# A list scheduler learns that GpSimd and VectorE take turns on two-input SBUF work, and the weight remainders go to VectorE alone

## The chip, the cores and the metric

One core of one Trainium2 chip runs the whole program in one launch. The metric is the device time in microseconds, median of the runs. Engines are named as the profile names them: PE is TensorE, DVE is VectorE, ACT is ScalarE, POOL is GpSimd and SP is SyncE, which here only issues the loads and stores.

## The reference

Two transformer-like blocks are computed in float32 for 256 tokens of 1024 features, with one set of weights each.

```
x = hybrid_layer(x, c, ...)        # block 1
h  = rmsnorm(x, g) * (1 + scale_m) + shift_m ; z = h @ w_in
merged = gate0 * (attention @ wa) + gate1 * (pool_mixer @ wb) + gate2 * (short_conv @ wc)
x = x + gate_m * rmsnorm(merged @ w_out)
x = x + gate_f * rmsnorm(square(relu(h2 @ w_ff1)) @ w_ff2)
...
x = second_block(x, mem, ...)      # block 2
y = concat(spatial_gating(za), moba_attention(q, k, v), conformer_conv(zc)) @ w_out
x = x + rms_norm(y); x = x + rms_norm(memory_cross_attention(...))
x = x + rms_norm(square(relu(h @ w_ff1)) @ w_ff2)
```

Some 160 MB of float32 weights pass through once.

## The kernel before, in words

**Products in three parts.** Each float32 factor is split into a rounded part `hi` (fp32r) and the exact remainder `lo`. A product is `xh*wh + xl*wh + xh*wl`, three matrix products into one PSUM bank. The tokens are two tiles of 128 rows, and the loops run over the tiles `t`, column chunks of 512, and k tiles of 128.

**Weights.** A weight unit is 128 x 1024 (two k tiles of 512 columns, 512 KB). SP loads it into a `raw` buffer, ACT makes `hi` by a copy, and `lo = raw - hi` is a subtraction of two SBUF inputs (`split_unit`). In the page these are `hi_w_...` and `lo_w_...`. Activations are split in the same way from PSUM (`evac_split`).

**The subtraction's engine.** In the kernel before, `split_unit` records the subtraction under `rec.either()`: it belongs to DVE, but POOL may take it where the scheduler finds POOL free long enough before it is due.

**What else is on DVE and POOL.** DVE sums the modulation rows (`G_a`, `S_a`, `GG_a`: 128 x 512 or 128 x 1024), does the attention's maxima, additions and normalisations (`alg`, `ap`, `bp`), the short convolution (`cy`), a part of the 31-tap convolution (`dy`), the residuals (`x0b`, `wG`) and the remainders of activations (`f1rT`, `kz`, `aPT`). POOL does each reciprocal root (`rstd`: an addition of eps, an addition, a power, on 128 x 1), the pooling windows (`s`, `pm`), 30 additions of the 31-tap convolution (`dy<-dy,tap`) and the additions to `merged`.

**What sets the order.** The program is recorded first (`Recorder`); `schedule` then plans thirty passes with a table of costs in microseconds and keeps the best, and each engine's instructions are issued in that fixed order. In `one_pass` every engine has a time at which it is free; an instruction can start when its inputs are made (plus a latency `LAT`), its engine is free, its buffers are free and its PSUM bank is not held. `urgency` turns the PE gaps of one pass into due times for the next. The engines run in order on the chip: what stands at the head of an engine's queue and waits holds up all behind it.

In the plan before, DVE and POOL never hold each other up: a subtraction on DVE is planned with 0.068 + 1024/960 us whatever POOL does. Nearly every instruction has line 1635 of the file in the profile, the line that issues them all, so rows are told apart by tile names.

Of the kernel before, what the change touches and what calls it, by code (L numbers as in the profile page):

```python
# [19 lines left out]
P = 128  # L20
D = 1024
# [23 lines left out]


def _chunk(rows, c, w, per):
    """One column chunk, `per` k tiles a unit."""
    return [(list(range(k, k + per)), c, w) for k in range(0, rows // P, per)]
# [6 lines left out]
def _ff2_units():  # L56
    """For each chunk of 512 rows both column halves."""
    return [([k, k + 1], c, 512) for g in range(8) for c in (0, 512) for k in (4 * g, 4 * g + 2)]
# [49 lines left out]
def _constants():  # L108
# [5 lines left out]
    # a pair of heads' rows of the running sums, and the even and the odd rows  # L114
# [5 lines left out]
    # slopes 2 ** -(h + 1) of a pair's heads: a diagonal times halved and quartered distances  # L120
# [17 lines left out]
class Buf:  # L138
    """A recorded tile; it takes a place of its tag when its first write is scheduled."""
# [11 lines left out]
class View:  # L151
    """A view of a recorded tile; `how` makes it from the tile's access pattern."""
# [17 lines left out]
    def cut(self, n):  # L170
        """the last axis as (axis, n)"""
        ids = self.ids.reshape(self.ids.shape[:-1] + (-1, n))
        if len(self.shape) == 2:
            return self._with(ids, lambda ap: ap.rearrange("p (k t) -> p k t", t=n))
        return self._with(ids, lambda ap: ap.rearrange("p a (k t) -> p a k t", t=n))

    def flat(self):
        """the last two axes as one"""
        ids = self.ids.reshape(self.ids.shape[:-2] + (-1,))
        return self._with(ids, lambda ap: ap.rearrange("p k t -> p (k t)"))  # L180

    def spread(self, shape):
        """stride 0 along the last axis, or along a new middle axis"""
# [14 lines left out]
class Pair:  # L198
    """The rounded part and the exact rest of values, as one index in the second place."""
# [9 lines left out]
class Wide:  # L209
    """Pairs of tiles of 4 k tiles each; one token tile of them."""  # L210
# [8 lines left out]
class At:  # L219
    """One token tile of a view whose last axis is the tokens."""  # L220
# [8 lines left out]
class Op:  # L229
    __slots__ = ("eng", "home", "due", "calls", "costs", "after", "prio", "waits", "ready", "users", "new", "bufs", "banks", "table", "end", "why", "start", "key", "goal", "mean", "boost", "freer")  # L230


class Recorder:
    """Engines whose calls are recorded with what they read and write, and a list
    scheduler that then emits them: each engine takes, of the instructions that are
    ready, the first in the recorded order (with its offset)."""

    # microseconds from the end on one engine to the start on another
    LAT = {"PE": 0.2, "ACT": 0.15, "DVE": 0.15, "POOL": 0.1, "SP": 0.9}
    TO_PE, LOOK, SWITCH = 0.12, 0.25, 1.28  # L240
    # the function tables that serve what not every table has
# [31 lines left out]
    def first(self):  # L273
        """what is recorded here goes ahead of all else, in its order"""
# [5 lines left out]
    def together(self):  # L280
        """products of one accumulation, issued without others between them"""
# [7 lines left out]
    def either(self):  # L289
        """for DVE, or for Pool when that has the time"""  # L290
# [12 lines left out]
    def add(self, eng, calls):  # L303
# [4 lines left out]
        op.costs = {e: sum(self.cost(e, *c) for c in calls) for e in ([eng, "POOL"] if self.flex else [eng])}  # L308
        after, bufs = {}, {}
# [29 lines left out]
        # no write to a tile before the one that takes its place  # L339
# [9 lines left out]
    def cost(self, eng, method, args, kw):  # L349
        """microseconds that an instruction holds its engine"""  # L350
        vs = [v for v in list(args) + list(kw.values()) if isinstance(v, View)]
        n = max(int(np.prod(v.shape[1:])) for v in vs) if vs else 1
        if eng == "PE":
            passes = 2 if method == "matmul" and kw["lhsT"].buf.dtype == F32 else 1
            return passes * (max(int(np.prod(vs[0].shape[1:])) / 2400, 0.107) + 0.0025)
        if eng == "SP":
            return vs[0].shape[0] * n * 4 / 3.6e5
        if eng == "ACT":
            ptr = sum(isinstance(kw.get(k), View) for k in ("bias", "scale", "accum_out"))
            return (0.052 if args[1].buf.tag == "ps" else 0.094) + n / 1200 + 0.093 * ptr  # L360
        if eng == "POOL":
            if method == "memset":
                return 0.035 + 0.000833 * n
            if method == "tensor_scalar":
                return 0.16 + 0.00116 * n
            if method == "tensor_copy":
                return 0.12 + 0.0033 * n
            return 0.3 + 0.165 * n if kw.get("op") == OP.pow else 0.15 + 0.0021 * n
        if method == "reciprocal":
            return 0.068 + 0.0063 * n  # L370
# [5 lines left out]
        return 0.068 + n / rate + 0.061 * ptr  # L376

    def schedule(self):
        """The recorded instructions in the order in which they are to be issued:
        the best of some passes, each with the urgencies that follow from the last."""  # L380
# [26 lines left out]
    def urgency(self, out):  # L407
        """latest starts with which PE would go without a gap; they order the other engines"""
        end = gap = 0.0
        for t, op in out:  # L410
            if op.home == "PE":
# [3 lines left out]
                if t - end > 0.1:  # L415
                    # the chain that PE has waited for goes sooner
# [31 lines left out]
    def one_pass(self):  # L448
        engs = list(self.real)
        free = {e: 0.0 for e in engs}  # L450
        dma_free, table = 0.0, ["exp"]
        slots = {tag: [(0.0, place, None, None) for place in places] for tag, places in self.slots.items()}
        pending = {t: list(o) for t, o in self.order.items()}
        todo = {e: [] for e in engs}  # all that came before is scheduled
# [9 lines left out]
        def placed(op):  # L464
            """when all new tiles of op can have a place, or None"""
            r, got = 0.0, {}
            for b in op.new:
                f, line = slots[b.tag], pending[b.tag]
                # every tile that comes before in the recorded order keeps a place
# [6 lines left out]
        def turn(op):  # L476
            """a bank of PSUM serves one engine at a time"""
            return max((t + lat(o, op.eng) for b in op.banks for o, t in b.held.items() if o != op.eng), default=0.0)

        while len(out) < len(self.ops):  # L480
            best = None
            for e in engs:
                cands = []
                for op in todo[e] if e != "SP" else sorted(todo[e], key=lambda o: o.key)[:24]:
                    r = placed(op) if op.new else 0.0
                    if r is not None:
                        cands.append((max(r, op.ready, free[e], turn(op)), op))
                if e == "POOL":
                    for op in todo["DVE"]:
                        if "POOL" in op.costs and op.due is not None:  # L490
                            r = max(placed(op) or 0.0, op.ready, free[e])
# [31 lines left out]
            else:  # L523
# [4 lines left out]
                op.end = free[e] = t + c  # L528
            op.start = t
# [18 lines left out]
def tile_two_blocks(ctx: ExitStack, tc: tile.TileContext, a: dict, out: bass.AP):  # L548
# [6 lines left out]
    # a pool for each place, so that the schedule says which one a tile takes  # L555
# [54 lines left out]
    def split_unit(raw, n, name, pieces=1):  # L610
        hi = work([P, D], "k4", f"hi_{name}", F32R)
        lo = work([P, D], "k4", f"lo_{name}", F32R)
        for i in range(pieces):
            s = slice(i * n // pieces, (i + 1) * n // pieces)
            act.activation(hi[:, s], raw[:, s], AF.Copy)
            with rec.either():
# [3 lines left out]
    # pieces of work that go between the weight units  # L620
# [31 lines left out]
    def use(u, xT, ps, first, last, xk=None, apart=False):  # L652
        """ps += x @ unit; xT(k) or xT [P, 2, k, P]"""
# [19 lines left out]
    def rstd(means, name, eps=None):  # L673
        """(the sum of the means + eps) ** -0.5"""
# [14 lines left out]
    def squares(parts, name):  # L689
        """each row's sum of squares over a piece, divided by the length D of the rows"""  # L690
# [8 lines left out]
    def evac_split(dst_hi, dst_lo, src, scale=None):  # L699
        """src (times scale) into its rounded part and the exact rest"""  # L700
# [14 lines left out]
    def to_T(src, dst, nb, name, scale=None):  # L715
        """src [P tok, nb*128] f32 -> dst [P, 2, nb, P]"""
# [5 lines left out]
    def to_T_gain(src, dst, g, name, halves=(0, 1)):  # L722
        """src [P tok, 1024], transposed, times g along the features -> dst"""
# [14 lines left out]
    # ================= start: mem, modulation =================  # L738
    mem = [work([P, 4, 256], "k4", f"mem{h}") for h in range(2)]  # features on the partitions
# [18 lines left out]
    # silu(c)  # L758
# [5 lines left out]
    # keys of one head keep only its half of a pair's rows; the other half stays zero  # L764
# [4 lines left out]
    def sums_on_partitions(src, n, name):  # L769
        """the sums of src's n * 128 columns over its partitions, on the partitions"""  # L770
# [11 lines left out]
    def mem_gain(k):  # L782
        """a k tile of both token tiles times its gains"""
# [4 lines left out]
    def mem_stats():  # L788
        """each token's mean square: over the k tiles first, then over the partitions"""
# [14 lines left out]
    def chunk(wname, u0, nu, xT, name, n=512, after=None):  # L804
        """x @ one column chunk for both token tiles, the first ahead of the second"""
# [35 lines left out]
    def mod_vector(j, name, gname=None, plus1=False, raw=None):  # L841
        """One of the six vectors on all partitions, as pieces of work: shift, or
        gate * g, or (1 + scale) * g. The partial sums of each partition's rows
        come first, then the sum over the partitions."""
# [40 lines left out]
    def mod_column(j, half, name, bias, gname=None):  # L885
        """half of the features of shift, or of (1 + scale) * g, on the partitions,
        as pieces of work"""
# [47 lines left out]
    def norm_shift(t, xG, r, S, name):  # L935
        """(xG * r + S) transposed and split; xG is overwritten"""
# [7 lines left out]
    # x * rstd(x) transposed, its first 512 features and its last  # L944
# [36 lines left out]
    # ================= block 1: w_in =================  # L981
    # forget gates and pooling input
# [28 lines left out]
    def log_sigmoid():  # L1011
        """min(z, 0) - log1p(u), u = exp(-|z|);
        log1p(u) = log(w) * u / (w - 1) with w = 1 + u, and u where w is 1"""
# [23 lines left out]
    def running_sums(t):  # L1037
        """cumq [token, head], and cumT [head, token] with the rounded parts in the
        first rows and the rest from row 32 on, even heads apart from odd"""
# [24 lines left out]
    def pooling(t):  # L1064
        """windowed sums by doubling, channels on partitions"""
# [57 lines left out]
    # the first chunks start with the features that are ready first  # L1123
# [157 lines left out]
    # ================= projections back to the residual =================  # L1281
    def proj(wname, xT, name, after, xk=None):
        """x @ w for 1024 columns, the first token tile ahead of the second"""
# [56 lines left out]
    def junction(t, y, x, G, g, name):  # L1340
        """x += G * y * rstd(y); (x * g) transposed and split, and rstd(x), which
        goes into the next outputs"""
# [343 lines left out]
```

## Time and profile before

| what | value |
|---|---|
| time, median of 3 runs | 862.42 us (861.46 to 863.27) |
| span of the profiled execution, first to last instruction | 856.9 us |
| median of the runs over that span | 5.5 us |
| PE busy | 790.5 us, 92% |
| DVE busy | 603.1 us, 70% |
| ACT busy | 482.2 us, 56% |
| POOL busy | 274.3 us, 32% |
| mean granted PE clock | 0.976 |
| HBM traffic | 163.64 MB read, 192 GB/s over the span |

The profiled execution's own total is not listed beside its span, so the three runs stand for it. A group's row reads: line, engine, operation, output<-inputs, shapes, count, then busy time and the mean of one in ns, then the idle time of the engine just before these instructions and who ended it.

### The profile page before, as it was taken

Reading aid. Unit: us, or ns where it says so; the run is one execution under the profiler, and the core shown is the slowest. Engines: PE = TensorE matmul, PEld = TensorE weight load, DVE = VectorE, ACT = ScalarE, POOL = GpSimd, SP = SyncE. Lnnn points to the kernel's source line nnn. Section 1 sums busy time; section 2 is a strip of 40 time slices with the busy share of each in tenths; the row PEclk is TensorE's granted clock in tenths of the full one; section 3 lists DMA queues with packets and bytes.
Section 4 is the critical chain, followed back from the end, with each engine's and each line's share of the span. In section 5 each row is a group of like instructions: output and inputs, shape, how many; then the busy total and the mean of one; then the engine's idle time right before and its main releaser. Section 6 shows DMA issues by size and latency. Waiting matters only on the chain.

```text
span 856.9 us, 10705 instructions
## 1 busy us (share of the span) xinstructions
PE 790.5 (92%) x3722; PEld 650.2 (76%) x3722; DVE 603.1 (70%) x814; ACT 482.2 (56%) x802; POOL 274.3 (32%) x227
## 2 busy tenths in 40 slices
PE   6998779999999789999999996879999999999997
PEld 4887667777877567888887785768787788888885
DVE  6798898977786986544454869898777954445413
ACT  6763745654454546555554785568576854545522
POOL 4143944543434544000000669364543400000000
PEclk9999999999999899999999999889999999999999
DMA  8998435556784566455556452314254555555511
GB/s 320 398 378 298 168 120 197 200 198 220 293 319 163 194 243 241 168 178 190 197 197 204 152 197 75 124 49 172 101 194 166 197 203 178 185 202 179 185 31 49
DMA packets 49630, 165.39 MB, mean 193 GB/s; under 512 B 5412, under 2 KB 6564, under 8 KB 49576
## 3 DMA queue, kind: packets, MB, share of 16 engines
q1 hardware_dynamic: 49576, 164.71, 54.7%
q8 instruction: 29, 0.48, 0.2%
q14 instruction: 25, 0.20, 0.1%
HBM read 163.64 MB, written 1.05 MB: 192 GB/s over the span
## 4 chain that ended last, share of the span: by engine, by line
PE 61%; DVE 19%; ACT 6%; DMA 5%; issue 5%; POOL 3%; SPq 0%; DVEq 0%; POOLq 0%; ACTq 0%
PE f2y L1635 10%; PE f2f L1635 10%; PE f1y L1635 9%; PE f1f L1635 8%; PE kv L1635 4%; PE wo L1635 3%; DMA raw_w_in<-in_w_in_dram 3%; DVE lo_w_in L1635 3%; PE bcg L1635 2%; DVE dy L1635 2%; PE xo L1635 2%; DVE GG_a L1635 2%; PE xq L1635 1%; PE xA L1635 1%; DVE G_a L1635 1%
## 5 line engine op out<-in xcount | busy, mean ns | idle before, releaser
L1635 DVE TENSOR_TENSOR lo_w_ff<-raw_w_ff,hi_w_ff 128x1024 fp32r<-128x1024 f32 x115 | 144.2, 1258 | 126.9 <-ACT hi_w_ff L1635 105.0
L1635 ACT ACTIVATE hi_w_ff<-raw_w_ff 128x1024 fp32r<-128x1024 f32 x128 | 134.7, 1061 | 109.6 <-DMA raw_w_ff<-in_w_ff_dram 78.4
L1635 POOL TENSOR_TENSOR lo_w_in<-raw_w_in,hi_w_in 128x1024 fp32r<-128x1024 f32 (+1 forms) x27 | 68.2, 2534 | 77.3 <-ACT hi_w_in L1635 42.3
L1635 PE MATMUL f1y<-hi_w_ff,f1rT 128*128 128x512 f32 x256 | 81.5, 399 | 3.4 <-DVE f1rT L1635 3.4
L1635 PE MATMUL f1f<-hi_w_ff,h2T 128*128 128x512 f32 x256 | 80.9, 397 | 0.3 <-DVE h2T L1635 0.3
L1635 ACT ACTIVATE hi_w_in<-raw_w_in 128x1024 fp32r<-128x1024 f32 (+1 forms) x66 | 67.3, 1035 | 24.2 <-DMA raw_w_in<-in_w_in_dram 16.3
L1635 PE MATMUL f2f<-hi_w_ff,h5T 128*128 128x512 f32 x256 | 80.0, 393 | 0.0
L1635 PE MATMUL f2y<-hi_w_ff,f2rT 128*128 128x512 f32 x256 | 79.6, 392 | 0.0
L1635 DVE TENSOR_TENSOR lo_w_in<-raw_w_in,hi_w_in 128x1024 fp32r<-128x1024 f32 (+1 forms) x39 | 64.5, 1661 | 7.5 <-ACT hi_w_in L1635 6.6
L1635 PEld LDWEIGHTS f1y<-hi_w_ff,f1rT 128*128 128x128 f32 x256 | 48.1, 191 | 13.9 <-DVE f1rT L1635 4.2
L1635 PEld LDWEIGHTS f1f<-hi_w_ff,h2T 128*128 128x128 f32 x256 | 48.0, 190 | 10.2 <-DVE h2T L1635 0.6
L1635 PEld LDWEIGHTS f2y<-hi_w_ff,f2rT 128*128 128x128 f32 x256 | 47.5, 188 | 9.4
L1635 PEld LDWEIGHTS f2f<-hi_w_ff,h5T 128*128 128x128 f32 x256 | 47.4, 188 | 9.5 <-DVE h5T L1635 0.2
L1635 POOL TENSOR_TENSOR o_m<-o_ss,e 128x1 f32<-128x1 f32 x2 | 0.4, 190 | 165.6 <-ACT junk L1635 165.6
L1635 PE MATMUL f1y<-lo_w_ff,f1rT 128*128 128x512 f32 x128 | 50.5, 394 | 0.0
L1635 PE MATMUL f1f<-lo_w_ff,h2T 128*128 128x512 f32 x128 | 50.1, 392 | 0.0
L1635 PE MATMUL f2f<-lo_w_ff,h5T 128*128 128x512 f32 x128 | 49.9, 390 | 0.0
L1635 PE MATMUL f2y<-lo_w_ff,f2rT 128*128 128x512 f32 x128 | 49.9, 390 | 0.0
L1635 PE MATMUL kv<-hi_w_xkv,memT 128*128 128x512 f32 x128 | 42.4, 414 | 5.8 <-ACT hi_w_xkv L1635 5.7
L1635 POOL TENSOR_TENSOR lo_w_ff<-raw_w_ff,hi_w_ff 128x1024 fp32r<-128x1024 f32 x13 | 35.5, 2739 | 34.8 <-ACT hi_w_ff L1635 27.3
L1635 PEld LDWEIGHTS kv<-hi_w_xkv,memT 128*128 128x128 f32 x128 | 24.3, 196 | 12.4 <-ACT hi_w_xkv L1635 6.4
L1635 POOL TENSOR_TENSOR wsf<-wsf,cstr 128x512 f32<-128x512 f32 x1 | 1.3, 1284 | 93.2 <-DMA wsf<-in_w_s_dram 93.2
(473 smaller groups left out, 1948.3 us busy)
## 6 DMA issues: line engine op xcount, KB each, us to landing
raw_w_ff<-in_w_ff_dram SPq DMA_DIRECT2D x128, 512.0 KB, 4.0
raw_w_in<-in_w_in_dram SPq DMA_DIRECT2D x62, 512.0 KB, 4.7
raw_GG<-in_w_ada_dram SPq DMA_DIRECT2D x16, 512.0 KB, 4.7
raw_w_out<-in_w_out_dram SPq DMA_DIRECT2D x16, 512.0 KB, 4.5
raw_w_xkv<-in_w_xkv_dram SPq DMA_DIRECT2D x15, 512.0 KB, 8.2
G<-in_w_ada_dram SPq DMA_DIRECT2D x8, 512.0 KB, 8.7
S<-in_w_ada_dram SPq DMA_DIRECT2D x8, 512.0 KB, 9.2
raw_w_branch<-in_w_branch_dram SPq DMA_DIRECT2D x8, 512.0 KB, 4.0
```

The costliest lines, as they stand in the source:

```text
L1635: getattr(rec.real[op.eng], method)(*map(out_of, args), **{k: out_of(v) for k, v in kw.items()})
```

## The change

The scheduler's costs are set anew, a port is added to its model, and `rec.either()` is replaced by `if True:`, so that every weight remainder is recorded for DVE. The lost comments and docstrings, which are most of the diff, change nothing and are left out.

```
-    LAT = {"PE": 0.2, "ACT": 0.15, "DVE": 0.15, "POOL": 0.1, "SP": 0.9}
-    TO_PE, LOOK, SWITCH = 0.12, 0.25, 1.28
+    LAT = {"PE": 0.2, "ACT": 0.14, "DVE": 0.12, "POOL": 0.12, "SP": 0.9}
+    TO_PE, LOOK, SWITCH = 0.03, 0.25, 1.28
...
+        op.port = {e: self.takes_port(e, *calls[0]) for e in op.costs}
...
-            return passes * (max(int(np.prod(vs[0].shape[1:])) / 2400, 0.107) + 0.0025)
+            return passes * max(int(np.prod(vs[0].shape[1:])) / 2400 + 0.0135, 0.109)
...
-            return 0.3 + 0.165 * n if kw.get("op") == OP.pow else 0.15 + 0.0021 * n
+            return 0.35 + 0.165 * n if kw.get("op") == OP.pow else 0.16 + 0.00216 * n
...
-        return 0.068 + n / rate + 0.061 * ptr
+        return 0.08 + n / rate + 0.061 * ptr
+
+    def takes_port(self, eng, method, args, kw):
+        if eng != "DVE":
+            return eng == "POOL"
+        ins = [v for k, v in [*enumerate(args[1:]), *kw.items()] if k != "accum_out" and isinstance(v, View)]
+        ins = [v for v in ins if int(np.prod(v.shape[1:])) > 1]
+        if any(v.buf.tag == "ps" for v in ins):
+            return False
+        return len(ins) > 1 or method in ("tensor_scalar", "tensor_copy")
...
+        port = {"DVE": 0.0, "POOL": 0.0}
+        other = {"DVE": "POOL", "POOL": "DVE"}
...
-                        cands.append((max(r, op.ready, free[e], turn(op)), op))
+                        p = port[other[e]] if op.port[e] else 0.0
+                        cands.append((max(r, op.ready, free[e], turn(op), p), op))
...
+                if op.port[e]:
+                    port[e] = op.end
...
-            with rec.either():
+            if True:
                 dve.tensor_sub(lo[:, s], raw[:, s], f(hi[:, s]))
```

The arithmetic and the loads are the same. POOL has 232 rows in the order before and 171 after; the 61 that go are the weight remainders. All engines are ordered anew. Three places show it.

On ACT in block 2, before: the last taps of the 31-tap convolution (`tap`), the weight copies, the split of the spatial gating's normalised input (`vr<-vn`), then the keys of the MoBA attention (`bkn<-bk`), which PE transposes next.

```order
L1635 ACTIVATE tap0_4_5050<-cx_3968,cols_406 128x256
L1635 ACTIVATE hi_w_in_218_5055<-raw_w_in_218_4941 128x1024
L1635 ACTIVATE hi_w_in_219_5071<-raw_w_in_219_4969 128x1024
L1635 ACTIVATE tap1_30_5083<-cx_3968,cols_406 128x256
L1635 ACTIVATE vr_5087<-vn0_5066 128x4x64
L1635 ACTIVATE vr_5087<-vn1_5069 128x4x64
L1635 ACTIVATE bkn0_5099<-bk0_4997,rz0_423 128x512
```

The same keys after:

```order
L1651 ACTIVATE tap0_4_5034<-cx_3968,cols_406 128x256
L1651 ACTIVATE bqT0_5038<-bqt0_4939 128x512
L1651 ACTIVATE tap1_27_5047<-cx_3968,cols_406 128x256
L1651 ACTIVATE bkn0_5057<-bk0_4974,rz0_423 128x512
L1651 ACTIVATE tap1_28_5068<-cx_3968,cols_406 128x256
```

`bkn` no longer stands behind the two `vr`, which are sixteen rows further down, behind the first attention exponentials.

On DVE in block 1, before: the remainders of the pooling (`pT<-pm`), then the short convolution (`cy`) with a weight remainder inside it.

```order
L1635 TENSOR_TENSOR pT_1411<-pm01_1379,pT_1411 128x128
L1635 TENSOR_TENSOR pT_1411<-pm10_1375,pT_1411 128x128
L1635 TENSOR_SCALAR cy0_1445<-cT_444,cols_406 128x128 x2
L1635 SCALAR_TENSOR_TENSOR cy0_1445<-cT_444,cols_406,cy0_1445 128x128
L1635 TENSOR_TENSOR lo_w_in16_1450<-raw_w_in16_1282,hi_w_in16_1434 128x1024
L1635 SCALAR_TENSOR_TENSOR cy0_1445<-cT_444,cols_406,cy0_1445 128x128 x3
L1635 TENSOR_TENSOR cy0_1445<-cy0_1445,cut0_1343 128x256
```

The same convolution after:

```order
L1651 TENSOR_TENSOR lf_420<-lgf_1334,lf_420 128x16
L1651 TENSOR_SCALAR cy0_1360<-cT_436,cols_406 128x128 x2
L1651 SCALAR_TENSOR_TENSOR cy0_1360<-cT_436,cols_406,cy0_1360 128x128 x4
L1651 TENSOR_TENSOR lo_w_in14_1380<-raw_w_in14_1201,hi_w_in14_1312 128x1024
L1651 TENSOR_SCALAR cy1_1391<-cT_436,cols_406 128x128 x2
L1651 SCALAR_TENSOR_TENSOR cy1_1391<-cT_436,cols_406,cy1_1391 128x128 x4
L1651 TENSOR_TENSOR cy0_1360<-cy0_1360,cut0_1338 128x256
```

The convolution moved ahead of the pooling's remainders, and weight remainders 14 to 19, of which POOL had 15, 17, 18 and 19, now stand on DVE around it.

On POOL at the end of the conformer convolution, before: the reciprocal root of its second token tile (`gr1_m0`, `gr1_r`) between weight remainders.

```order
L1635 TENSOR_TENSOR lo_w_out_22_5273<-raw_w_out_22_5236,hi_w_out_22_5264 128x1024
L1635 TENSOR_TENSOR lo_w_out_24_5348<-raw_w_out_24_5320,hi_w_out_24_5332 128x1024
L1635 TENSOR_SCALAR gr1_m0_5388<-gvs1_5383 128x4
L1635 TENSOR_TENSOR gr1_r_5394<-gr1_m0_5388,mhalf_407 128x4
L1635 TENSOR_TENSOR lo_w_out_23_5418<-raw_w_out_23_5275,hi_w_out_23_5385 128x1024
L1635 TENSOR_TENSOR lo_w_out_26_5455<-raw_w_out_26_5373,hi_w_out_26_5426 128x1024
```

The same place after:

```order
L1651 TENSOR_SCALAR gr0_m0_5287<-gvs0_5277 128x4
L1651 TENSOR_TENSOR gr0_r_5293<-gr0_m0_5287,mhalf_407 128x4
L1651 TENSOR_SCALAR gr1_m0_5336<-gvs1_5327 128x4
L1651 TENSOR_TENSOR gr1_r_5341<-gr1_m0_5336,mhalf_407 128x4
L1651 TENSOR_SCALAR h4y0_m0_5694<-h4y0_ss0_5680 128x1
```

Nothing long is left on POOL there.

More of the change, by code (lines that the diff above doesn't have):

```diff
@@ L229 @@
 class Op:
-    __slots__ = ("eng", "home", "due", "calls", "costs", "after", "prio", "waits", "ready", "users", "new", "bufs", "banks", "table", "end", "why", "start", "key", "goal", "mean", "boost", "freer")
+    __slots__ = ("eng", "home", "due", "calls", "costs", "after", "prio", "waits", "ready", "users", "new", "bufs", "banks", "table", "end", "why", "start", "key", "goal", "mean", "boost", "freer", "port")
 class Recorder:
-    LAT = {"PE": 0.2, "ACT": 0.15, "DVE": 0.15, "POOL": 0.1, "SP": 0.9}
-    TO_PE, LOOK, SWITCH = 0.12, 0.25, 1.28
+    LAT = {"PE": 0.2, "ACT": 0.14, "DVE": 0.12, "POOL": 0.12, "SP": 0.9}
+    TO_PE, LOOK, SWITCH = 0.03, 0.25, 1.28
     TABLES = {AF.Exp: ["exp"], AF.Tanh: ["exp", "gelu"], AF.Ln: ["ln"], AF.Gelu: ["gelu"]}
@@ L359, in cost @@
             ptr = sum(isinstance(kw.get(k), View) for k in ("bias", "scale", "accum_out"))
-            return (0.052 if args[1].buf.tag == "ps" else 0.094) + n / 1200 + 0.093 * ptr
+            return (0.065 if args[1].buf.tag == "ps" else 0.113) + n / 1200 + 0.088 * ptr
         if eng == "POOL":
             if method == "memset":
-                return 0.035 + 0.000833 * n
+                return 0.06 + 0.000833 * n
             if method == "tensor_scalar":
@@ L366, in cost @@
             if method == "tensor_copy":
-                return 0.12 + 0.0033 * n
-            return 0.3 + 0.165 * n if kw.get("op") == OP.pow else 0.15 + 0.0021 * n
+                return 0.12 + 0.0012 * n
+            return 0.35 + 0.165 * n if kw.get("op") == OP.pow else 0.16 + 0.00216 * n
         if method == "reciprocal":
-            return 0.068 + 0.0063 * n
+            return 0.075 + 0.0063 * n
         rate, ptr = 960, 0
@@ L490, in one_pass @@
                         if "POOL" in op.costs and op.due is not None:
-                            r = max(placed(op) or 0.0, op.ready, free[e])
+                            r = max(placed(op) or 0.0, op.ready, free[e], port["DVE"])
                             end = r + op.costs[e]
```

## The prediction

> **What bounds the kernel now.** I read the page first, then the busy time by stage, then what PE waits for, and last the places of its longest waits in the order of time. On the page, PE is the fullest engine by far and most of the chain that ended last:
>
> ```profile
> PE 790.5 (92%) x3722; PEld 650.2 (76%) x3722; DVE 603.1 (70%) x814; ACT 482.2 (56%) x802; POOL 274.3 (32%) x227
> PE 61%; DVE 19%; ACT 6%; DMA 5%; issue 5%; POOL 3%; SPq 0%; DVEq 0%; POOLq 0%; ACTq 0%
> ```
>
> PE's work is not changed, so only its idle time, 856.9 - 790.5 = 66.4 us, and the time at a reduced clock can be won. The busy time by stage (start and end, length, then busy us and count of PE, PEld, DVE, ACT, POOL, and the granted PE clock) tells where that lies:
>
> ```profile
> 64.00:160.00 96.00, 81.75 (x420) 68.46 (x419) 87.81 (x152) 50.45 (x97) 51.16 (x39) 0.96 0.54 187
> 160.00:265.00 105.00, 96.69 (x442) 78.91 (x441) 84.78 (x110) 52.07 (x81) 45.63 (x21) 0.98 0.67 241
> 265.00:315.00 50.00, 42.09 (x183) 33.71 (x182) 43.57 (x37) 26.06 (x41) 25.90 (x19) 0.93 0.61 221
> ...
> 315.00:470.00 155.00, 153.21 (x694) 126.10 (x693) 81.60 (x73) 80.19 (x97) 9.96 (x5) 0.99 0.58 199
> ...
> 500.00:605.00 105.00, 90.17 (x433) 74.86 (x432) 93.76 (x176) 75.03 (x167) 66.75 (x62) 0.92 0.32 111
> ...
> 680.00:857.00 177.00, 170.68 (x782) 141.01 (x780) 78.21 (x75) 80.86 (x103) 1.84 (x6) 0.99 0.45 152
> ```
>
> The two feed-forward layers (315 to 470, 680 to 857) leave nothing. The four other stages shown hold 14.3 + 8.3 + 7.9 + 14.8 = 45.3 us of PE idle time, and in them DVE is busy for 81 to 91%. Who PE waits for (us in total, times, longest):
>
> ```profile
> PE bkt L1635 <- ACT bkn L1635: 9.3, 1, 9.3
> ...
> PE aA L1635 <- DVE ap L1635: 5.5, 3, 2.0
> PE h_t L1635 <- DVE wG L1635: 4.7, 3, 2.8
> PE aqt L1635 <- ACT aqn L1635: 4.5, 1, 4.5
> PE wo L1635 <- DVE ybT L1635: 4.0, 1, 4.0
> ...
> PE f1y L1635 <- DVE f1rT L1635: 3.4, 2, 3.0
> PE G L1635 <- DVE G_a L1635: 2.8, 1, 2.8
> PE po L1635 <- DVE pT L1635: 1.9, 1, 1.9
> ```
>
> These eight rows are 36.1 us. The place of the 4.5 us wait shows their common cause. In the timelines of POOL and of DVE (start, length, engine, operation, count):
>
> ```profile
> 104.84 8.14 POOL L1635 TENSOR_TENSOR lo_w_in<-raw_w_in,hi_w_in 128x1024 fp32r<-128x1024 f32 x3 [1.17 <-ACT hi_w_in L1635]
> ```
>
> ```profile
> 104.91 3.42 DVE L1635 TENSOR_TENSOR lo_w_in<-raw_w_in,hi_w_in 128x1024 fp32r<-128x1024 f32 x1
> 108.25 5.14 DVE L1635 SCALAR_TENSOR_TENSOR cy<-cT,cols,cy 128x128 f32<-128x128 f32 x3
> ...
> 114.16 1.13 DVE L1635 SCALAR_TENSOR_TENSOR cy<-cT,cols,cy 128x128 f32<-128x128 f32 x4
> ...
> 115.73 1.28 DVE L1635 SCALAR_TENSOR_TENSOR GG_a<-raw_GG,csil,GG_a 128x1024 f32<-128x1024 f32 x1
> ```
>
> Three `cy` take 5.14 us while POOL makes three weight remainders, and four take 1.13 us once POOL is done. A DVE instruction with two SBUF inputs waits for the whole POOL instruction. ACT's split of `cy` waits for that, `aqn` stands behind it on ACT, and PE waits for `aqn`. The plan knew nothing of this.
>
> **The change part by part.** *The remainders that move.* Of the 61, POOL's two largest groups show a mean of 2.5 to 2.7 us, and DVE's own remainders a median of 1.225 us (count, then min/median/max in ns):
>
> ```profile
> L1635 POOL TENSOR_TENSOR lo_w_in<-raw_w_in,hi_w_in 128x1024 fp32r<-128x1024 f32 (+1 forms) x27 | 68.2, 2534 | 77.3 <-ACT hi_w_in L1635 42.3 <-PE aA L1635 11.6 <-PE bbg L1635 11.3
> L1635 POOL TENSOR_TENSOR lo_w_ff<-raw_w_ff,hi_w_ff 128x1024 fp32r<-128x1024 f32 x13 | 35.5, 2739 | 34.8 <-ACT hi_w_ff L1635 27.3 <-PE f1f L1635 4.6 <-DMA raw_w_ff<-in_w_ff_dram 2.8
> ```
>
> ```profile
> L1635 DVE TENSOR_TENSOR lo_w_ff<-raw_w_ff,hi_w_ff x115: 1209/1225/2582, 266.3 to 818.8; 128x1024 fp32r<-128x1024 f32 x115
> ```
>
> DVE is given 61 x 1.225 = 74.7 us. It gets back the time for which its instructions now wait under POOL's remainders. Five groups bound that from below:
>
> ```profile
> L1635 DVE TENSOR_TENSOR lo_w_ff<-raw_w_ff,hi_w_ff 128x1024 fp32r<-128x1024 f32 x115 | 144.2, 1258 | 126.9 <-ACT hi_w_ff L1635 105.0 <-PE f2y L1635 11.0 <-PE f1y L1635 9.5
> ...
> L1635 DVE TENSOR_TENSOR lo_w_in<-raw_w_in,hi_w_in 128x1024 fp32r<-128x1024 f32 (+1 forms) x39 | 64.5, 1661 | 7.5 <-ACT hi_w_in L1635 6.6 <-issue 0.6
> ...
> L1635 DVE SCALAR_TENSOR_TENSOR GG_a<-raw_GG,csil,GG_a 128x1024 f32<-128x1024 f32 x16 | 27.1, 1692 | 2.0 <-DMA raw_GG<-in_w_ada_dram 1.7
> ...
> L1635 DVE TENSOR_TENSOR f1rT<-f1s,f1rT 128x512 fp32r<-128x512 f32 x16 | 17.6, 1100 | 4.8 <-ACT f1rT L1635 4.7
> ...
> L1635 DVE TENSOR_SCALAR ap<-ap,arc 128x128 f32<-128x128 f32 (+1 forms) x16 | 13.0, 827 | 0.4
> ...
> L1635 DVE TENSOR_TENSOR f2rT<-f2s,f2rT 128x512 fp32r<-128x512 f32 x16 | 11.1, 692 | 24.8 <-ACT f2rT L1635 24.7
> ```
>
> ```profile
> 166.40 0.38 DVE L1635 TENSOR_SCALAR ap<-ap,arc 128x256 f32<-128x256 f32 x1
> ```
>
> `lo_w_in`: 64.5 - 39 x 1.225 = 16.7. `lo_w_ff`: 144.2 - 115 x 1.225 = 3.3. `GG_a`: 27.1 - 16 x 1.28 = 6.6. `f1rT` against `f2rT`, the same sixteen instructions in the layer where POOL has almost nothing: 6.5. `ap`: 13.0 - 16 x 0.38 = 6.9. That is 40 us. So DVE's load grows by at most 74.7 - 40 = 35 us; the groups that I did not count were held up too, and if they make up the rest it does not grow. I take a third, some 10 us: DVE about as full as before, its instructions short again.
>
> The Trainium skill has a rule against moving work this way: in Perfetto Trace Analysis, Identifying the Most-Contended Engine, the engine with the highest occupancy is the one to relieve, and DVE is fuller than POOL here. The same page, Optimizing Scalar/DVE Operations, says that the two share an SBUF port, so that offloading between them might not help; the `cy` rows agree. By the first rule the sum would be that of the first rival below.
>
> *PE's waits.* What each of the eight rows keeps is my choice, from the length of the instructions behind it.
> - `ap` (5.5): 2.4 us instead of 0.38 before each wait; keeps 1.5, gives 4.0.
> - `aqn` (4.5): in the new order `cy` is ahead of the pooling and the POOL remainders are gone; keeps 0.5, gives 4.0.
> - `f1rT` (3.4) and `wG` (4.7): the same waits beside `lo_w_ff` on POOL, but the modulation sums `GG_a` stay in this stage; keep 0.9 and 1.5, give 2.5 and 3.2.
> - `G_a` (2.8) and `pT` (1.9): keep 1.3 and 0.9, since `lo_w_in` remainders now stand between the sums; give 1.5 and 1.0.
> - `ybT` (4.0): it stands on DVE behind the conformer's normalisation, of which this row is the first of three,
>
> ```profile
> 563.34 2.59 DVE L1635 TENSOR_TENSOR gxc<-gxc,gr_r 128x256 f32<-128x256 f32 x1 [0.27 <-POOL gr_r L1635]
> ```
>
> held up by two remainders on POOL. The power and the tanh behind it stay on the path: gives 2.0.
> - `bkn` (9.3): it stands on ACT behind `vr`, which waits for `vn`:
>
> ```profile
> ACT vr L1635 <- DVE vn L1635: 7.6, 2, 5.5
> ```
>
> ```profile
> L1635 POOL TENSOR_TENSOR dy<-dy,tap 128x256 f32<-128x256 f32 x30 | 26.2, 875 | 7.5 <-ACT tap L1635 5.6
> ```
>
> The new order has `bkn` ahead of `vr`, so this wait goes. Next late are the spatial gating and the convolution, for POOL's 30 additions stay, still hold up DVE, and end no sooner. I take 6.0 of 9.3.
>
> Sum: 4.0 + 4.0 + 2.5 + 3.2 + 1.5 + 1.0 + 2.0 + 6.0 = 24.2 us.
>
> *The clock.* Behind the long waits PE runs slowly (same columns as above, clock third from the end):
>
> ```profile
> 117.00:120.50 3.50, 3.50 (x12) 2.93 (x12) 3.43 (x4) 3.50 (x5) 0.00 (x0) 0.57 0.00 0
> ...
> 291.00:297.50 6.50, 4.87 (x17) 4.12 (x18) 6.46 (x6) 3.27 (x5) 2.18 (x1) 0.50 0.31 84
> ...
> 538.00:542.50 4.50, 4.33 (x15) 3.76 (x16) 4.45 (x10) 2.90 (x6) 0.00 (x0) 0.50 0.11 19
> 568.80:573.00 4.20, 4.13 (x12) 3.38 (x13) 4.07 (x16) 3.89 (x11) 2.47 (x2) 0.50 0.01 2
> ```
>
> PE's busy time there at the lost share of the clock is 3.50 x 0.43 + (4.87 + 4.33 + 4.13) x 0.50 = 8.2 us. Where the wait shrinks below about 2 us I count the loss as gone; that holds for most, so 6 us. The skill's TensorE: Matmul & The Clock Gate, What's actually happening, states that the clock halves after an idle window of about 3.4 us. By it the wait of 2.8 us ahead of the second row would cost no clock and the term would be about 2 us less; the row has 0.50 there, so it counts here.
>
> *What is added.* Each remainder on DVE stands in front of short instructions for up to 1.2 us, and POOL's three short instructions per reciprocal root must now wait for a port that DVE uses more:
>
> ```profile
> L1635 POOL TENSOR_SCALAR h4x_m<-h4x_ss x2: 247/1227/2207, 593.5 to 610.0; 128x1 f32<-128x1 f32 x2
> ```
>
> One such instruction of 128 x 1 took 247 ns and its twin 2207 ns. Some twenty roots (two token tiles of each normalisation in the code) are on a chain to PE. The bounds are a gain of 5 us (two remainders of 2.5 us less on POOL ahead of a root) and a loss of 25 us (one more DVE remainder, 1.225 us, for each root). I take a loss of 6. The other edits of the cost table change what the plan believes by hundredths to tenths of a microsecond an instruction and have no price of their own. SP's loads keep their order nearly; DMA is 5% of the chain, and I count nothing.
>
> In all 24.2 + 6 - 6 = 24.2 us: a span of 832.7 us, and with the 5.5 us between span and median 838 us.
>
> **The rivals.** *DVE becomes the bound (slower).* Outside the feed-forward stages DVE is busy for 603.1 - 81.6 - 78.2 = 443.3 of 525 us. With 74.7 more, and S us of waiting returned, it reaches the 91% of its fullest stage at S = 443.3 + 74.7 - 0.91 x 525 = 40 us. Below that every microsecond lengthens these stages: with S = 25 they last 493 / 0.91 = 542 us, 17 us more, which gives 879 us. It decides if POOL's remaining work holds DVE up as much as the remainders did, above all from 500 to 605 us. Against it, my five groups alone give 40.
>
> *The waits only change places.* The chains of roots, tanh and transposes are as long as before, and a third of the 24.2 us is won; 8 - 6 = 2 us gives 860 us. For it: the conformer's and the attention's chains remain, and PE has the same work to put between them.
>
> *Nearly all waits go.* 36.1 + 8.2 - 6 = 38 us gives 824 us. Against it: DVE stays above 80% in four stages.
>
> *The planner's turns are not the chip's.* If short instructions slip in between, the new order plans waits that don't occur, and half is won: 850 us. Against it: `cy` and `ap` waited whole instructions.
>
> **How the numbers follow.** Forecast 0.58, in its own range 828 to 850; waits change places 0.17; DVE the bound 0.10; nearly all 0.10; turns not the chip's 0.05. The likeliest case gives 838 us. From 824 to 861 the range leaves out the slower rival, half of the best one and a little of the 860 us one. 0.2% is 1.7 us, about what three runs can tell from no change. Faster: 0.58 + 0.10 + 0.05 and 0.08 of the 860 us case, 0.81. Same: 0.05 of that case. Slower: its last 0.04 and 0.10, 0.14.
>
> **What the profile after would show.** DVE's `lo_w_in` mean at 1.25 us or so, and `ap`, `f1rT`, `GG_a` at 0.4, 0.7 and 1.3; DVE busy near 610 us, POOL near 274.3 - 61 x 2.5 = 122; no wait of PE for `bkn` or `aqn` above 3 us; PE idle near 40 us and the clock near 0.985. I am wrong if DVE is above 92% in the stages from 64 to 315 us and PE's waits for it are no shorter, or if PE's waits reappear under other names with the same sum.

## The result and the profile after

| what | before | after |
|---|---|---|
| time, median of four runs | 861.94 us (860.75 to 863.27) | 828.67 us (824.79 to 832.42) |
| span of the profiled execution | 856.9 us | 830.6 us (its own time 832.42) |
| PE idle in that span | 66.4 us | 42.9 us |

The ratio after to before is 0.962, with a 95% interval of 0.958 to 0.966: faster by 33 us. The page of the kernel after, engines and then the chain that ended last:

```profile
PE 787.7 (95%) x3722; PEld 648.0 (78%) x3722; DVE 578.9 (70%) x875; ACT 483.1 (58%) x802; POOL 116.3 (14%) x166
PE 81%; DVE 7%; DMA 6%; ACT 3%; issue 2%; SPq 0%; POOL 0%; DVEq 0%; POOLq 0%; ACTq 0%
```

DVE issues 61 instructions more than before (875 against 814) and is busy for 24 us less. POOL is emptied as the count says, and the chain is PE for 81% instead of 61%. The busy time by stage (same columns), cut where PE has begun about as many matmuls as at the cuts shown of before, but for the cut at 64 us:

```profile
64.00:145.00 81.00, 80.87 (x447) 69.43 (x446) 76.38 (x161) 53.78 (x100) 15.51 (x26) 1.00 0.69 238
145.00:246.00 101.00, 96.25 (x442) 79.25 (x442) 85.74 (x123) 50.59 (x79) 13.96 (x9) 0.97 0.68 246
246.00:293.00 47.00, 42.78 (x184) 34.15 (x183) 38.73 (x43) 25.35 (x41) 7.04 (x13) 0.93 0.69 238
...
478.00:582.00 104.00, 92.24 (x434) 73.79 (x433) 89.00 (x188) 76.20 (x166) 43.82 (x51) 0.97 0.34 114
```

PE's idle time in these four stages is 0.1 + 4.8 + 4.2 + 11.8 = 20.9 us, where it was 45.3. The first 64 us, before and after, show what the cut there hides:

```profile
0.00:64.00 64.00, 56.96 (x271) 46.20 (x272) 49.74 (x64) 44.69 (x70) 22.13 (x28) 1.00 0.98 365
```

```profile
0.00:64.00 64.00, 54.30 (x245) 43.34 (x246) 50.47 (x71) 42.86 (x67) 14.38 (x23) 0.97 0.95 352
```

PE has begun 26 matmuls fewer there and is idle for 9.7 us instead of 7.0. So the first stage shown gave most, 14.1 us, though 2.7 us of it were lost ahead of its start. It is also the one in which DVE is fullest: 76.38 of 81 us, 94%. The fullness of an engine did not decide; how long its single instructions hold up a chain did. What PE waits for after the change:

```profile
PE kv L1651 <- ACT hi_w_xkv L1651: 6.8, 2, 5.1
PE f1t L1651 <- ACT f1r L1651: 4.8, 4, 2.4
PE wo L1651 <- ACT mT L1651: 3.5, 1, 3.5
PE sg L1651 <- ACT vr L1651: 3.3, 1, 3.3
PE kv L1651 <- DVE memT L1651: 2.0, 1, 2.0
PE h_t L1651 <- DVE wG L1651: 1.9, 1, 1.9
...
PE dyt L1651 <- DVE dy L1651: 1.4, 1, 1.4
...
PE f1y L1651 <- DVE f1rT L1651: 0.2, 1, 0.2
...
PE wo L1651 <- DVE ybT L1651: 0.2, 1, 0.2
```

Of the eight waits that the prediction summed (36.1 us), three are left, `wG`, `f1rT` and `ybT`, with 2.3 us. Others have grown: `f1r` (1.4 us before), `mT` and `vr` on ACT. The largest, `kv` at the start of the program, was there before with 5.7 us. The groups of DVE:

```profile
L1651 DVE TENSOR_TENSOR lo_w_ff<-raw_w_ff,hi_w_ff 128x1024 fp32r<-128x1024 f32 x128 | 156.7, 1231 | 134.3 <-ACT hi_w_ff L1651 110.7 <-PE f2y L1651 11.2 <-PE f1y L1651 7.4
L1651 DVE TENSOR_TENSOR lo_w_in<-raw_w_in,hi_w_in 128x1024 fp32r<-128x1024 f32 (+1 forms) x66 | 79.6, 1228 | 19.8 <-ACT hi_w_in L1651 18.5 <-PE bcg L1651 0.7 <-PE glup L1651 0.5
...
L1651 DVE SCALAR_TENSOR_TENSOR GG_a<-raw_GG,csil,GG_a 128x1024 f32<-128x1024 f32 x16 | 20.6, 1290 | 0.1
...
L1651 DVE TENSOR_TENSOR f1rT<-f1s,f1rT 128x512 fp32r<-128x512 f32 x16 | 11.1, 692 | 3.5 <-ACT f1rT L1651 3.4
...
L1651 DVE TENSOR_SCALAR ap<-ap,arc 128x128 f32<-128x128 f32 (+1 forms) x16 | 4.7, 314 | 0.1
```

Each of these groups now has a mean near its undisturbed length: 1.23 us for a remainder, 0.692 us for `f1rT`, the same as `f2rT` had before.

### The profile page after: what moved, and what is told of

Read it like the earlier page. It is cut to its first block, busy times and chain, and to the rows that moved or that the text cites. A ratio compares the mean times of both kernels' runs of the same rounds, so it can differ in the third digit from the quotient of the medians.

```text
span 830.6 us, 10599 instructions
## 1 busy us (share of the span) xinstructions
PE 787.7 (95%) x3722; PEld 648.0 (78%) x3722; DVE 578.9 (70%) x875; ACT 483.1 (58%) x802; POOL 116.3 (14%) x166
## 4 chain that ended last, share of the span: by engine, by line
PE 81%; DVE 7%; DMA 6%; ACT 3%; issue 2%; SPq 0%; POOL 0%; DVEq 0%; POOLq 0%; ACTq 0%
PE f2f L1651 11%; PE f2y L1651 11%; PE f1y L1651 9%; PE f1f L1651 9%; PE wo L1651 4%; PE kv L1651 4%; PE bbg L1651 3%; PE bcg L1651 3%; PE xo L1651 3%; PE xq L1651 2%; PE bag L1651 2%; DMA raw_w_in<-in_w_in_dram 2%; PE aA L1651 2%; PE hb L1651 1%; PE ak L1651 1%
## 5 line engine op out<-in xcount | busy, mean ns | idle before, releaser
L1651 DVE TENSOR_TENSOR lo_w_ff<-raw_w_ff,hi_w_ff 128x1024 fp32r<-128x1024 f32 x128 | 156.7, 1231 | 134.3 <-ACT hi_w_ff L1651 110.7
L1651 DVE TENSOR_TENSOR lo_w_in<-raw_w_in,hi_w_in 128x1024 fp32r<-128x1024 f32 (+1 forms) x66 | 79.6, 1228 | 19.8 <-ACT hi_w_in L1651 18.5
L1651 POOL TENSOR_TENSOR dy<-dy,tap 128x256 f32<-128x256 f32 x30 | 27.5, 918 | 10.8 <-ACT dy L1651 8.7
L1651 PEld LDWEIGHTS f1y<-lo_w_ff,f1rT 128*128 128x128 f32 x128 | 24.7, 193 | 5.4
L1651 PEld LDWEIGHTS f1f<-lo_w_ff,h2T 128*128 128x128 f32 x128 | 24.5, 191 | 5.3
L1651 PEld LDWEIGHTS f2y<-lo_w_ff,f2rT 128*128 128x128 f32 x128 | 24.0, 188 | 5.1
```

What stands on the lines that cost most here:

```text
L1651: getattr(rec.real[op.eng], method)(*map(out_of, args), **{k: out_of(v) for k, v in kw.items()})
```

## The experiments

The change has three parts: the remainders on DVE alone, the turns in the planner's clock, and the new cost table. Theory A says that the gain is POOL's remainders out of DVE's way; B that it is the turns; C that it is the table. Four kernels take parts out of the change. The first has the remainders alone:

```
 (kernel before)
-            with rec.either():
+            if True:
                 dve.tensor_sub(lo[:, s], raw[:, s], f(hi[:, s]))
```

> The kernel before with one of the three parts of the change alone: every weight remainder is recorded for DVE, and the planner keeps its old costs and knows no turns. Theory A (the gain is POOL's 61 remainders taken out of the way of DVE's two-input work, and their own waiting with them): nearly all of the measured gain of 33 us comes with this part, so 828 to 836 us, DVE busy about 580 us as after, POOL about 116. Theory B (the gain is that the planner sets the order with turns in its clock): this part alone gives little, 850 to 862 us, and long PE waits for DVE stay, since DVE is given 61 more operations of 1.23 us and the plan is no truer. Theory C (the gain is the cost table): 850 to 862 us as well.

Measured: 816.55 us, ratio to before 0.947 (0.944 to 0.950). That is 12 us better than the whole change, below even what A expected. Its page:

```profile
PE 782.9 (96%) x3722; PEld 647.5 (79%) x3722; DVE 583.0 (72%) x875; ACT 480.7 (59%) x802; POOL 121.6 (15%) x166
```

The kernel after without the turns:

```
-                if op.port[e]:
-                    port[e] = op.end
```

> The kernel after, without the turns in the planner: new costs and remainders on DVE alone. Theory A: 826 to 832 us, as after, for with the remainders gone from POOL there is little left to take turns over. Theory B: 840 to 855 us, and the PE waits for DVE tiles that the plan takes for early come back. Theory C: 826 to 832 us.

Measured: 828.26 us, 0.962 (0.958 to 0.966), the same as the kernel after. B falls: what the planner knows of turns is worth nothing that can be measured once POOL makes no remainders.

The kernel after with `LAT`, `TO_PE` and `cost` as before:

> The kernel after with the old cost table: turns in the planner and remainders on DVE alone. Theory A: 828 to 836 us. Theory B: 828 to 836 us. Theory C: 845 to 862 us, since the planner takes PE work and POOL's operations for other than they are.

Measured: 817.54 us, 0.948 (0.945 to 0.951). C falls too, and to the other side: the new table costs 11 us, with turns in the plan as without (816.55 us above against 828.26).

The kernel after in which POOL may take remainders again:

```
-            if True:
+            with rec.either():
                 dve.tensor_sub(lo[:, s], raw[:, s], f(hi[:, s]))
```

> The kernel after with the planner again free to give a remainder to POOL: new costs, turns in the clock. It gives POOL 44 of them instead of 61 of before. Theory A: a POOL remainder still costs DVE and itself, so 44/61 of the loss is back: of 33 us some 24, so 845 to 855 us, with DVE busy about 575 to 595 us (44 operations fewer of 1.23 us, 54 us, but the waiting back), and POOL about 220. Theory B: the planner puts them where their turns harm nobody: 825 to 835 us. Theory C: 825 to 835 us.

Measured: 854.48 us, 0.991 (0.988 to 0.995), as A said. The page has DVE at 584.3 us although it issues 44 instructions fewer than after:

```profile
PE 799.9 (94%) x3722; PEld 655.9 (77%) x3722; DVE 584.3 (68%) x831; ACT 481.9 (56%) x802; POOL 232.8 (27%) x210
```

The next kernel adds the load without giving DVE anything back, in the order of the kernel after. LOADED are the units that POOL made before:

```
+            if b is not None and b.name in LOADED and method == "tensor_sub":
+                again = f(args[0].real())
+                nc.gpsimd.tensor_sub(args[1].real(), again, again)
```

> The kernel after, plan and order unchanged, with 61 subtractions more on POOL: for the same units that POOL made before, POOL subtracts the finished remainder from itself into the raw tile, which is dead by then. Nobody reads what they write, only the raw tile comes free later, and the output stays the same. So PE waits for none of them, and what they cost comes from DVE's and POOL's turns, from POOL's queue and from the later raw tiles. Theory A (the remainders on POOL cost by being there): DVE busy rises from 579 by 50 to 80 us, to 630 to 660, the time from 828 by 15 to 33 us, to 843 to 861. Theory D (what counts is that PE no longer waits for a remainder made slowly on POOL, and the order of the plan): DVE busy may rise, but the time by less than 8 us, 828 to 836.

Measured: 888.82 us, 1.033 (1.031 to 1.036): 60 us more than the kernel after, so more than A expected. Its page, one of its POOL groups, a DVE group, and waits of PE:

```profile
PE 806.9 (91%) x3722; PEld 659.2 (74%) x3722; DVE 625.6 (71%) x875; ACT 483.0 (54%) x802; POOL 250.4 (28%) x227
```

```profile
L1666 POOL TENSOR_TENSOR raw_w_in<-lo_w_in 128x1024 f32<-128x1024 f32 (+1 forms) x27 | 63.4, 2353 | 103.6 <-DVE lo_w_in L1662 53.1 <-issue 9.1 <-PE aq L1662 7.7
```

```profile
L1662 DVE TENSOR_TENSOR lo_w_in<-raw_w_in,hi_w_in 128x1024 fp32r<-128x1024 f32 (+1 forms) x66 | 91.4, 1407 | 19.2 <-ACT hi_w_in L1662 15.1 <-POOL raw_w_in L1666 3.6 <-POOL dy L1662 0.4
```

```profile
PE aA L1662 <- DVE ap L1662: 6.6, 3, 3.3
...
PE h_t L1662 <- DVE x0b L1662: 5.3, 3, 3.0
...
PE f1y L1662 <- DVE f1rT L1662: 4.6, 2, 4.3
PE h_t L1662 <- DVE wG L1662: 4.0, 1, 4.0
```

PE waits for none of the 61, and yet the waits of before are back: `ap`, `f1rT`, `wG`. DVE's busy time rose by 46.7 us, a little less than the 50 to 80 that A expected. PE's idle time rose from 42.9 to 886.6 - 806.9 = 79.7 us, and its own busy time by 19.2 us, the granted clock being 0.958 instead of 0.982.

To part the streaming from the places in POOL's queue, the same 61 with one element a partition:

```
-                nc.gpsimd.tensor_sub(args[1].real(), again, again)
+                nc.gpsimd.tensor_sub(args[1].real()[:, 0:1], again[:, 0:1], again[:, 0:1])
```

> The loaded kernel (888.8 us) with its 61 extra POOL subtractions cut to one element of each partition: they stand at the same places of POOL's queue, wait for the same remainders and hold the same raw tiles, but move next to nothing. Theory A1 (the streaming of 1024 elements, in turns with DVE, costs the 60 us): 828 to 840 us. Theory A2 (POOL's queue behind an instruction that waits for DVE, and the raw tiles that come free late, cost it): 855 to 889 us.

Measured: 830.20 us, 0.964 (0.961 to 0.967), not to be told from the kernel after. The rows:

```profile
PE 788.3 (95%) x3722; PEld 648.6 (78%) x3722; DVE 579.4 (70%) x875; ACT 482.2 (58%) x802; POOL 145.7 (18%) x227
```

```profile
L1666 POOL TENSOR_TENSOR raw_w_in<-lo_w_in 128x1 f32<-128x1 f32 x27 | 18.1, 671 | 116.0 <-DVE lo_w_in L1662 57.9 <-issue 10.4 <-DVE arc L1662 9.5
```

```profile
L1662 DVE TENSOR_TENSOR lo_w_in<-raw_w_in,hi_w_in 128x1024 fp32r<-128x1024 f32 (+1 forms) x66 | 78.9, 1216 | 17.6 <-ACT hi_w_in L1662 16.4 <-PE glup L1662 0.5 <-POOL dy L1662 0.4
```

The same instructions at the same places cost nothing when they are short, so the 59 us between the two kernels are the length of the subtractions on POOL: the turns with DVE, and what waits behind 2.3 us instead of 0.7 us for POOL's results or for the tiles it holds. No run parts these, but the waits of the two kernels say that all of them grew: DVE and ACT wait 20.6 us instead of 7.5 for POOL's other results (roots, pooling, additions), 13.0 us instead of 0.7 until one of the 61 has ended, and DVE is busy for 46 us more. PE's waits for weight tiles are 8.5 us against 7.6, so late loads hardly reach it directly.

Now the move without a new plan. The kernel before, its own plan, but each instruction issued on the engine it was recorded for:

```
+        op.eng = op.home
```

> The kernel before with its own plan and order, but the 61 remainders that this plan had for POOL are issued on DVE, each at the place that the plan gave it; the plan isn't made anew. Theory A: turns and POOL's queue are gone though the order is that of before: DVE busy falls from 603 to about 580 us though it has 61 operations more, and the time falls by 15 to 33 us, to 829 to 847. Theory D (a new order is needed for it): DVE's order has no room for them, the PE waits for DVE tiles stay or grow, 855 to 880 us.

Measured: 828.85 us, 0.963 (0.960 to 0.965). The old order holds as much as the whole change gained. A plan made anew around the moved remainders, with the old costs, is worth 12 us more: that is the first experiment, 816.55 us. Its page, and the waits that remain:

```profile
PE 781.8 (95%) x3722; PEld 643.8 (78%) x3722; DVE 581.3 (71%) x875; ACT 480.5 (58%) x802; POOL 117.6 (14%) x166
```

```profile
PE bkt L1636 <- ACT bkn L1636: 7.2, 1, 7.2
...
PE aA L1636 <- DVE ap L1636: 2.3, 2, 1.4
PE po L1636 <- ACT pT L1636: 2.2, 1, 2.2
PE h_t L1636 <- DVE wG L1636: 2.2, 3, 1.6
```

`aqn`, `f1rT` and `G_a` are gone without a new order, and `ap`, `wG` are halved. `bkn` stays: that one wait does come from the order. It is not what the time hangs on, for the first experiment is faster than the kernel after although PE waits 6.2 us for `bkn` in it. The same plan on both sides gives the cleanest price of a remainder on POOL: DVE was busy 603.1 us with 814 instructions, and without POOL's remainders they would have taken about 581.3 - 74.7 = 506.6 us, so it waited 96.5 us more, or 96.5 / 61 = 1.58 us for each remainder that POOL took off it. To make it itself takes DVE 1.225 us.

Would turns in the plan save a shared division? The kernel before with the port in its planner, and `LAT`, `TO_PE`, `cost` and `rec.either()` as before:

> The kernel before with the turns alone in the planner's clock: old costs, and a remainder may still go to POOL, which gets 50 of them instead of 61. Each remainder on POOL has cost (862.0 - 816.6) / 61 = 0.74 us so far. Theory A (a remainder on POOL costs wherever it is put): 816.6 + 50 x 0.74 = 854, so 848 to 860 us. Theory B (a plan that knows the turns puts them where they harm nobody): 820 to 840 us.

Measured: 852.88 us, 0.990 (0.987 to 0.993), inside A's span and far from B's. By A's price, eleven remainders fewer on POOL are worth 8 us, and the kernel before, run beside this one, took 860.59 us, 7.7 more: no gain is left for the turns.

The 11 us of the cost table could be an unlucky order. Two kernels change the planner's look-ahead, a number without meaning on the chip:

```
-    TO_PE, LOOK, SWITCH = 0.03, 0.25, 1.28
+    TO_PE, LOOK, SWITCH = 0.03, 0.26, 1.28
```

> The kernel after with one number of the planner changed that stands for nothing on the chip: it looks 0.26 us ahead instead of 0.25, and so finds another order. If the orders of one planner scatter little, 825 to 832 us, and the 11 us between the kernel after (828) and the old costs (817) belong to the costs. If the new costs merely came upon an unlucky order, anything from 815 to 840 us.

Measured: 826.54 us, 0.961 (0.958 to 0.964). And the same with old costs and no turns:

> Old costs, no turns, remainders on DVE alone (816.6 us) with the same look ahead of 0.26 us. If the orders scatter little, 813 to 820 us, and the new costs are what costs 11 us; if they scatter by ten, anything from 810 to 830 us.

Measured: 812.80 us, 0.945 (0.942 to 0.947), the fastest kernel here. The two pairs of orders of one table lie 2 and 4 us apart (828.7 and 826.5, 816.6 and 812.8), so the table's 11 us are hardly an accident of one order. Two runs look for the part of the table that costs them. First the kernel after with the old `cost` and the new `LAT` and `TO_PE`:

> The kernel after with the old durations of instructions, but with the new hand-over times from engine to engine (0.12 us after DVE instead of 0.15, 0.03 more to PE instead of 0.12). Theory H (the shorter hand-over times cost the 11 us between 828 and 817: the plan leaves PE's operands no slack): 824 to 832 us. Theory K (the new durations do): 813 to 820 us.

Measured: 818.18 us, 0.952 (0.949 to 0.955): the durations, not the hand-over times. Then the kernel after with PE's line alone as before:

```
-            return passes * max(int(np.prod(vs[0].shape[1:])) / 2400 + 0.0135, 0.109)
+            return passes * (max(int(np.prod(vs[0].shape[1:])) / 2400, 0.107) + 0.0025)
```

> The kernel after with one line of its durations as before, that of PE: 0.216 us for a matmul of 512 columns, where the trace has one start every 0.227 us, which is what the new line gives. Theory P (the old line makes the plan take PE for 5% faster than it is, so that it wants every operand earlier, and that slack is worth the 11 us): 814 to 820 us, as with all the old durations (818.2). Theory R (it is another of the new durations, on DVE, ACT or POOL): 825 to 831 us, as the kernel after.

Measured: 827.47 us, 0.962 (0.960 to 0.964). PE's line is not it, and theory P falls. All the orders planned with the old durations and with the remainders on DVE lie at 812.8 to 818.2 us (four kernels), all with the new ones on ACT, DVE and POOL at 826.5 to 828.7 (four, with the kernel after). Which of these three engines' lines it is, or whether several act together, and why, stays open.

## Why the prediction was right, and where its sizes were off

**Sign and mechanism.** The sign and the cause came as forecast, the time at the lower edge of the forecast case's own range (828 to 850): 838 us forecast, 828.67 measured, nearer to the 824 us of *nearly all waits go*. POOL's long instructions held up DVE's short ones, and those PE; the loaded kernel and its small twin show that cause, and the moved kernel that it needs no new order. DVE's means are where the prediction put them (`ap` 0.31, `f1rT` 0.69, `GG_a` 1.29 us), POOL is at 116 us (122 forecast), PE idle 42.9 us (40), the clock 0.982 (0.985), and PE has no wait for `bkn` or `aqn`.

**Where it was luck.** The gain of 33 us is what is left of larger terms: the move alone gives as much (828.85 us), a plan made anew around it gives 12 us more (816.55), and the new cost table takes 11 back. I had the table at nothing; with the old one the time would have been 816.55 or 817.54 us, below the whole range of 824 to 861. Inside the sum, PE's idle time fell by 5.3 us more than the net forecast and the clock gave 3.2 us less, so these two cancelled in part as well.

**The way from span to time: 7.4 of the 9.5 us.** The forecast before rounding was 832.7 + 5.5 = 838.2 us, 9.5 above the median. The sum ended at a span of 832.7 us, and 830.6 was profiled. Then I added 5.5 us, the distance from the profiled span of before to the median. An execution of the kernel after takes 832.42 - 830.6 = 1.8 us beyond its span. The other 3.7 us say only that the profiled execution of before was among its quicker ones; they were no property to carry over. The profiled execution of after was the slowest of its four, which made the miss larger.

**PE's waits.** The eight rows gave 36.1 - 2.3 = 33.8 us, not 24.2. But PE's idle time fell by 23.5 us only, so 10.3 us net came up elsewhere, above all `f1r` +3.4, `mT` on ACT 3.5 and `vr` 3.3. My shares for what each wait would keep held in the sum alone: I kept 11.9 us on these eight tiles, and 2.3 + 10.3 = 12.6 stayed, mostly on others. It would have been truer to take the waits as gone and to price the next late tile. At `bkn` I had named it: behind the 9.3 us came the gating (`vr`, 3.3) and the convolution (`dy`, 1.4), so 4.6 us net for the 6.0 taken. I credited the new order with `aqn`'s wait as well as POOL; the moved kernel shows no such wait in the old order.

**The clock: 2.8 us instead of 6.** PE's busy time fell from 790.5 to 787.7. The waits that came up have slow stretches behind them like the old ones (clock third from the end):

```profile
237.00:240.00 3.00, 2.92 (x8) 2.33 (x9) 3.00 (x4) 2.52 (x4) 2.13 (x1) 0.50 0.11 37
...
282.00:285.00 3.00, 3.00 (x8) 2.35 (x8) 2.31 (x3) 0.19 (x1) 0.00 (x0) 0.50 0.84 276
...
528.00:531.00 3.00, 3.00 (x15) 3.00 (x16) 2.53 (x12) 0.42 (x1) 1.17 (x2) 0.50 0.00 0
```

They follow the waits for `mT` (3.5 us), `wG` (1.9) and `vr` (3.3). I had counted the loss as gone where a wait falls below 2 us; the middle row has 0.50 behind 1.9 us and the eight short transposes that followed (1.29 us).

**DVE: the term that was most off.** I gave DVE 74.7 us and took 65 as returned, for a busy time near 610. Returned were 603.1 + 74.7 - 578.9 = 98.9 us. My five groups make up 41.3 of these (16.6 + 3.4 + 6.5 + 6.5 + 8.3), so the bound of 40 was sound; the rest, which I took at 25 us, was 57.6, more than the bound itself. Two of many such groups, before:

```profile
L1635 DVE TENSOR_TENSOR gxc<-gxc,v 128x256 f32<-128x256 f32 x4 | 5.8, 1449 | 0.1
L1635 DVE TENSOR_TENSOR vn<-vn,v 128x256 f32<-128x256 f32 x4 | 5.1, 1344 | 0.0
```

and after:

```profile
L1651 DVE TENSOR_TENSOR gxc<-gxc,v 128x256 f32<-128x256 f32 x4 | 1.7, 426 | 0.1
L1651 DVE TENSOR_TENSOR vn<-vn,v 128x256 f32<-128x256 f32 x4 | 1.6, 422 | 0.1
```

The number could have been had nearly whole beforehand: summed over all its instructions, DVE's time above the tenth percentile of the same operation, tiles and shape is 106 us in the profile of before, and 20 us after.

**What is added.** Against the loss of 6 us taken here, PE's idle time fell by 23.5 us where 24.2 - 6 = 18.2 was the net forecast, so a loss of this size doesn't show, and no run prices it alone. The roots on POOL do wait longer (last section), but PE's table has no row for them. The sentence that the other edits of the cost table "have no price of their own" is the step that failed outright: they cost 11 us, the price of the new table in two pairs of kernels (817.5 against 828.7 with turns, 816.6 against 828.3 without); with the new hand-over times alone (818.2) the loss is gone, so it lies in the durations.

**The rivals.** *DVE becomes the bound* was to decide below 40 us of returned time; 98.9 came back. Its price took 91% as the most that DVE can be busy; the stage from 64 to 145 us runs at 94% with PE idle for 0.1 us. *Waits only change places* happened for 10 of 34 us. *Nearly all waits go* came true of the eight rows, 33.8 of 36.1 us, but not of the clock, and its 824 us are closer to the result than my 838; DVE did stay above 80% in the four stages, but that did not keep the waits. *The planner's turns are not the chip's* was wrong in its price: a plan without turns loses nothing here. What helps is not that the plan knows the turns but that nothing long is left to take turns with.

**The two rules.** To optimize the engine with the highest occupancy first is the advice of the Trainium skill, Perfetto Trace Analysis, Identifying the Most-Contended Engine. As a rule against handing DVE more work it did not hold here: DVE was fuller than POOL, got 61 instructions more, and its busy time fell by 24 us, because 96.5 us of it had been waiting. The Trainium skill, SBUF — State Buffer, SBUF: two separate sides, says that of DVE and GpSimd the one that starts first has the shared pair of ports for its whole instruction, and that the other blocks. The trace of before agrees: the first two of the three `cy` that took 5.14 us lasted 2.48 and 2.47 us, and each ended 0.14 or 0.15 us after a remainder on POOL; undisturbed they take 0.34.

## What to carry to other kernels

Price work handed to POOL by what it costs DVE in waiting, from the spread of DVE's own instructions (group mean against the shortest of its form), and not by DVE's busy share: here POOL's help cost DVE 1.58 us for each 1.225 us that it saved. When a change has several parts, look for the one that does it alone: one line of this change gains 45 us, and a table of durations made anew gives 11 of them back. A planner's table is to be judged by the time of the kernel: here the orders made with the new durations were slower, and nothing found so far says why.

## What the runs showed of the hardware that was not expected

Not only instructions with two wide inputs wait for POOL. `ap`, a TENSOR_SCALAR with one (128 x 256), took up to 2.43 us before, beside a remainder on POOL, and at most 0.36 us after.

The turns are not even. Under three POOL remainders in a row, DVE's instructions in the rows of before got in between, one after each. The other way round POOL is sometimes kept out for longer. In the kernel after, POOL's addition of eps on 128 x 1, and DVE beside it:

```profile
570.85 3.33 POOL L1651 TENSOR_SCALAR h4x_m<-h4x_ss 128x1 f32<-128x1 f32 x1 [3.23 <-ACT junk L1651]
```

```profile
570.63 3.49 DVE L1651 TENSOR_TENSOR lo_w_xq<-raw_w_xq,hi_w_xq 128x1024 fp32r<-128x1024 f32 x3
574.04 0.60 DVE L1651 SCALAR_TENSOR_TENSOR h4T<-h_t,cols,h4T 128x128 fp32r<-128x128 f32 x2
```

The one-element instruction began 0.22 us into the first of three remainders and ended at 574.18 us, 0.06 us after the third (574.12), though two remainders began after it. Its twin, 2.95 us, and this one are the slowest of their form:

```profile
L1651 POOL TENSOR_SCALAR h4x_m<-h4x_ss x2: 2947/3136/3325, 570.8 to 585.5; 128x1 f32<-128x1 f32 x2
```

It is no rule. In the same kernel another POOL addition on 128 x 1 began under the second of five remainders and ended 0.05 us after that one, with three still to come:

```profile
642.22 0.53 POOL L1651 TENSOR_TENSOR h5y_m<-h5y_m,h5y_ss 128x1 f32<-128x1 f32 x1 [3.47 <-ACT junk L1651]
```

```profile
640.35 5.76 DVE L1651 TENSOR_TENSOR lo_w_ff<-raw_w_ff,hi_w_ff 128x1024 fp32r<-128x1024 f32 x5
```

Over all the traces of this case, 89 such POOL instructions (128 x 1) began under a DVE remainder with at least one more right behind it: 55 got in after the remainder under which they began, 34 only when the run of remainders had ended, the longest after 6.75 us, and none in the middle. What decides between the two stays open. PE's table of the kernel after has no row in which it waits for such a root.
